# The last row tile of an encoder block: its last columns in two quarters, its last sum of squares on Vector, its scaling on three engines

## The chip, the cores and the metric

The kernel runs on one core of one Trainium2 chip. A core has five engines that run side by side, each with an instruction queue of its own: TensorE (PE; its weight loads are shown as PEld), VectorE (DVE), ScalarE (ACT), GpSimd (POOL) and SyncE (SP), which here only issues DMAs. ACT and POOL issue DMAs too. Engines wait for each other through semaphores. Matrix products go to PSUM, a small memory of eight banks (2 KB per partition each); all else is in SBUF, with 128 partitions.

The metric is the device time of one execution in microseconds, the median over runs. The kernel before takes 2623.02 us (three runs, 2622.14 to 2624.28).

## The reference

One encoder layer is applied to 512 prompt rows and 256 sample rows of width 2048. After a Fourier group, windowed attention, an output projection and a residual add comes the part that matters here:

```
h = rmsnorm(x, ln_mlp_g)
u = relu(h @ w_up)
x = x + (u * u) @ w_down        # w_down: 8192 x 2048
y = rmsnorm(x, ln_final_g)      # x * rsqrt(mean(x*x) + eps) * g
```

The last norm needs the sum of squares of a whole row of 2048 before any element of that row can be scaled.

## The kernel before

The 768 rows are six row tiles of 128 (`NM`). Everything is fp32; each matrix product is made of three fp32r products (high by high, high by low, low by high), since each factor is split into a high and a low part. The up and down projections use seven half-size products in place of eight (Strassen's scheme). For the down projection the list `dunits` has two halves `kh` of the inner dimension, seven products `i` in the order (4, 2, 6, 0, 1, 3, 5) and eight steps `j` each: 112 units. A unit multiplies three row tiles (m = 0, 1, 2) by 1024 columns, 12 matmuls of 512 columns for each m, into three PSUM tiles `ps` of two banks each. The pool of PSUM tiles has four such buffers.

TensorE's order is that of the program. The orders on the other engines, and the waits, come from a framework that follows the program's order where it can and adds a semaphore wait where data or a buffer needs one. PSUM is tracked by bank: a matmul into a bank waits for the reads of that bank that stand before it.

- `products` (L1343) issues the matmuls of one unit and one row tile; `start` and `stop` are set on the first and last of the group of eight steps.
- `lows` (L1337) and `sums` (L1319) prepare a unit's factors on Vector and Scalar one and two units ahead; `loads` (L1310) puts its DMAs on SP three units ahead.
- `evacuate` (L1428) adds a PSUM tile into `acc`, the result so far: one scalar_tensor_tensor on Vector (L1434), acc = ps * rm + acc. `acc4(m, n)` is row tile m, columns 512n to 512n + 511. `acc[r][0]` holds the left 1024 columns and `acc[r][1]` the right ones.
- `square` (L1268) is Scalar's Square with a sum along the row into `ssy`; `gains` (L1272) multiplies by `gf` (ln_final_g) on Vector.
- `row_factor` (L1277) reduces the four sums of a row tile on Vector, then `rsqrt_of` (L92) scales and adds eps on Vector (L94) and raises to the power -0.5 on GpSimd (L97).
- `put` (L1281) scales 512 columns, on Scalar (L1284) where the gain is already in and on Vector with `gf` (L1286) where it isn't, and issues the DMA of the result (L1289).

The final product (kh = 1, i = 5) changes only the right 1024 columns of row tiles 3, 4 and 5; the left columns of those are finished earlier, squared and multiplied by the gain beside the matmuls of the units before (`beside`, L1297). In the last two units the products of m = 2 are held back: after m = 0 and m = 1 of the last unit come 24 matmuls of 512 columns for m = 2 (L1442 to L1445), 12 for columns 1024 to 1535 and then 12 for 1536 to 2047. Behind them stands the tail, written out as a list (L1447): evacuate and square the two column blocks of a row tile, form its row factor, put its four blocks. The four result blocks of the last row tile go out by GpSimd's queue (columns 0 to 511), Scalar's (512 to 1023) and SP's (the two right ones). The framework ends the program with a drain of every engine and a barrier (shown at L1524, the line of the framework's context).

Of the kernel before, what the change touches and what calls it, by code (L numbers as in the profile page):

```python
# [11 lines left out]
F32 = mybir.dt.float32  # L12
# [8 lines left out]
P = 128  # L21
# [19 lines left out]
def hybrid_encoder(ctx: ExitStack, tc: tile.TileContext, a: dict):  # L41
# [1230 lines left out]
    def gains(m, n):  # L1272
        nc.vector.tensor_tensor(
            out=acc4(m, n), in0=acc4(m, n), in1=ep["gf"][:, n * 512 : (n + 1) * 512], op=ALU.mult
        )

    def row_factor(m):  # L1277
        nc.vector.tensor_reduce(out=ry[:, m : m + 1], in_=ssy[:, m * 4 : m * 4 + 4], op=ALU.add, axis=AX.X)
        rsqrt_of(ry[:, m : m + 1], ry[:, m : m + 1], D, 1)
# [62 lines left out]

    def products(u, ps, m, cols=range(2)):  # L1343
        _, i, j = dunits[u]
        (sh, sl, _), whl = parts[u]
        for n in cols:
            for q in range(2):
                ts, ns = slice(m * P, (m + 1) * P), slice(n * 512, (n + 1) * 512)
                wh, wl, _ = whl[q]
                for t, (l, w) in enumerate(((sh, wh), (sh, wl), (sl, wh))):  # L1350
                    nc.tensor.matmul(  # L1351
                        ps[m][:, ns], l[:, q, ts], w[:, ns],
                        start=(j == 0 and q == 0 and t == 0), stop=(j == HP // 2 - 1 and q == 1 and t == 2),
                    )
# [55 lines left out]
    for u, (kh, i, j) in enumerate(dunits):  # L1410
# [27 lines left out]
        for m in range(3 if u > 0 else 0):  # L1438

            if not (final and j >= HP // 2 - 2 and m == 2):  # L1440
                products(u, ps, m)
        if final and last:  # L1442
            for n in range(2):
                for v in (u - 1, u):
                    products(v, ps, 2, (n,))  # L1445

            for what, m, q in (  # L1447
# [3 lines left out]
            ):  # L1451
                if what == "e":
                    evacuate(m, q - 2)
                    square(3 + m, q)
                elif what == "r":
                    row_factor(3 + m)
                else:
                    put(3 + m, q, q < 2, {(2, 0): nc.gpsimd, (2, 1): nc.scalar}.get((m, q), nc.sync))
            parts.clear()
# [69 lines left out]
```

## Time and profile before

| | |
|---|---|
| median of three runs | 2623.02 us (2622.14 to 2624.28) |
| the profiled execution's own time | 2622.38 us |
| its span, first to last instruction | 2620.3 us |
| mean granted TensorE clock | 0.998 |
| busy PE / DVE / ACT / POOL | 99% / 66% / 41% / 10% |
| start of the last matmul | 2609.21 us of the span |
| from the end of the last matmul to the end of the span | 10.7 us |

The page of the profile gives busy times, a chain of waits followed back from the last instruction, and groups of like instructions. The timeline lists instructions in order of time: start, duration, engine, line, operation, out<-in, shape and type, how many merged into the row (x2: start of the first, time to the end of the last), and in brackets how long the engine was idle before and who ended it. A row with q behind the engine's name (SPq, POOLq) is that of its sequencer: it issues a DMA, waits or drains. Consecutive instructions of an engine overlap by some 0.08 us, so two of 0.75 us take 1.41 us together.

### The profile page before, as it was taken

To read this page: it belongs to the slowest core of one execution; us is meant where nothing else is said; L and a number is where in the kernel's file an instruction comes from. 1 tells how busy PE (TensorE), PEld (TensorE's weight loads), DVE (VectorE), ACT (ScalarE), POOL (GpSimd) and SP (SyncE) were. 2 spreads that over 40 slices of the span, in tenths; PEclk is the share of its full clock that TensorE was granted. 3 is DMA by queue.
4 is the path that set the end of the run, shared out by engine and by line. 5 is a ranking of instruction groups with operands and counts; after the bars stand their busy time and mean duration, and the time that the engine had idled before them with its cause. 6 is when DMAs were issued, how large, how long until landed. Compare 5 with 4: busy or idle time off the path is not lost.

```text
span 2620.3 us, 35122 instructions
## 1 busy us (share of the span) xinstructions
PE 2600.0 (99%) x13680; PEld 2378.5 (91%) x13680; DVE 1736.2 (66%) x2176; ACT 1075.8 (41%) x1543; POOL 251.8 (10%) x354
## 2 busy tenths in 40 slices
PE   9999999999999999999999999999999999999998
PEld 9999998887889999999999999988888888888886
DVE  6334447776655655555777777757776765777687
ACT  6233327775333333333454445433333333333335
POOL 1011212333210111000000000010000000000001
PEclk9999999999999999999999999999999999999999
DMA  5323466444673554456666666685543672555364
GB/s 179 120 94 111 136 216 181 117 121 145 208 240 137 174 179 162 155 202 232 208 227 213 220 228 225 208 324 181 184 157 110 211 246 78 178 179 162 98 210 147
DMA packets 254982, 465.16 MB, mean 178 GB/s; under 512 B 20080, under 2 KB 151712, under 8 KB 254176
## 3 DMA queue, kind: packets, MB, share of 16 engines
q1 hardware_dynamic: 189536, 304.24, 36.7%
q10 hardware_dynamic: 53376, 110.97, 11.2%
q0 software_dynamic: 11904, 47.72, 5.4%
q8 instruction: 107, 1.75, 0.3%
q14 instruction: 59, 0.48, 0.1%
HBM read 344.10 MB, written 118.75 MB: 177 GB/s over the span
## 4 chain that ended last, share of the span: by engine, by line
PE 75%; DVE 1%; DMA 1%; issue 0%; ACT 0%; POOL 0%; POOLq 0%; ACTq 0%; SPq 0%; DVEq 0%
PE pu L966 35%; PE pd L1351 34%; PE pm L821 5%; PE ptx L130 0%; DMA sr<-sd 0%; DMA sd<-sm 0%; DMA oar<-oad 0%; DVE sr L760 0%; POOL p L676 0%; DVE acc L1434 0%; ACT oar L756 0%; DVE wl L1340 0%; DVE os L720 0%; DVE tl L692 0%; DVE o L987 0%
## 5 line engine op out<-in xcount | busy, mean ns | idle before, releaser
L966 PE MATMUL pu<-xf,wh 128*128 128x384 f32 x3072 | 783.2, 336 | 0.0
L966 PEld LDWEIGHTS pu<-xf,wh 128*128 128x128 f32 x3072 | 554.6, 188 | 1.5 <-ACT o L984 0.8
L1351 PE MATMUL pd<-wh,sl 128*128 128x512 f32 x1332 | 518.3, 389 | 0.4 <-DVE sl L1341 0.4
L1351 PE MATMUL pd<-wh,sh 128*128 128x512 f32 x1332 | 518.2, 389 | 0.0
L1351 PE MATMUL pd<-wl,sh 128*128 128x512 f32 x1332 | 518.2, 389 | 0.0
L966 PE MATMUL pu<-xf,wl 128*128 128x384 f32 x1536 | 516.1, 336 | 0.0
L1330 ACT ACTIVATE wh<-rd 128x1024 fp32r<-128x1024 f32 x200 | 202.3, 1054 | 522.8 <-PE pd L1351 425.8
L1340 DVE TENSOR_TENSOR wl<-rd,wh 128x1024 fp32r<-128x1024 f32 x200 | 236.0, 1221 | 226.8 <-ACT wh L1330 226.1
L946 ACT ACTIVATE wh<-ur 128x1024 fp32r<-128x1024 f32 x160 | 169.9, 1062 | 372.5 <-PE pu L966 210.7
L1351 PEld LDWEIGHTS pd<-wh,sl 128*128 128x128 f32 x1332 | 250.1, 188 | 52.5 <-DVE sl L1341 0.8
L1351 PEld LDWEIGHTS pd<-wh,sh 128*128 128x128 f32 x1332 | 250.1, 188 | 51.9
L1351 PEld LDWEIGHTS pd<-wl,sh 128*128 128x128 f32 x1332 | 250.1, 188 | 51.9
L966 PEld LDWEIGHTS pu<-xf,wl 128*128 128x128 f32 x1536 | 288.8, 188 | 0.0
L952 DVE TENSOR_TENSOR wl<-ur,wh 128x1024 fp32r<-128x1024 f32 x160 | 195.4, 1222 | 76.2 <-ACT wh L946 76.2
L987 DVE TENSOR_TENSOR o<-pu,o 128x768 f32<-128x768 f32 x160 | 152.8, 956 | 122.5 <-PE pu L966 114.9
L588 PE MATMUL pz<-hh,wh 128*128 128x384 f32 x576 | 147.1, 336 | 0.0
L588 PE MATMUL pz<-hl,wh 128*128 128x384 f32 x576 | 146.3, 334 | 0.0
L588 PE MATMUL pz<-hh,wl 128*128 128x384 f32 x576 | 146.3, 334 | 0.0
L1323 DVE TENSOR_TENSOR rd<-rd 128x1024 f32<-128x1024 f32 x112 | 131.7, 1217 | 0.0
L966 PE MATMUL pu<-xs,wh 128*128 128x384 f32 x512 | 130.4, 336 | 0.0
L946 ACT ACTIVATE wh<-sx 128x1024 fp32r<-128x1024 f32 x64 | 67.9, 1062 | 130.4 <-PE pu L966 105.6
L66 DVE TENSOR_TENSOR wl<-raw,wh 128x1024 fp32r<-128x1024 f32 x56 | 68.3, 1225 | 69.4 <-ACT wh L65 69.1
(228 smaller groups left out, 3725.3 us busy)
## 6 DMA issues: line engine op xcount, KB each, us to landing
rd<-in_w_down SPq DMA_DIRECT2D x176, 512.0 KB, 5.1
ur<-in_w_up SPq DMA_DIRECT2D x128, 512.0 KB, 3.9
sr<-sd SPq DMA_DIRECT2D x95, 384.0 KB, 5.3
pd<-o ACTq DMA_DIRECT2D x60, 384.0 KB, 2.3
o<-pd POOLq DMA_DIRECT2D x60, 384.0 KB, 5.8
sd<-sm ACTq DMA_DIRECT2D x60, 384.0 KB, 2.9
raw<-in_w_in SPq DMA_DIRECT2D x40, 512.0 KB, 3.6
raw<-in_w_out SPq DMA_DIRECT2D x32, 512.0 KB, 4.5
```

The lines of the kernel that those rows point to most:

```text
L66: nc.vector.tensor_tensor(out=lo, in0=src, in1=f32(hi), op=ALU.subtract)
L588: nc.tensor.matmul(ps[c][s][:, :HALF], w[:, i, cs], h[j][:, i, s * HALF : (s + 1) * HALF], start=first and n == 0, stop=stop and n == 2,)
L821: nc.tensor.matmul(ps, l(k), w[:, k % 2, :], start=(k == 0 and n == 0), stop=(k == 7 and n == 2))
L946: nc.scalar.activation(wh[:], raw[:], AF.Copy)
L952: nc.vector.tensor_tensor(out=wl[:], in0=raw[:], in1=f32(wh[:]), op=ALU.subtract)
L966: nc.tensor.matmul(ps[:, t, :HALF], w[:, i, t * P : (t + 1) * P], xb[:, o, i, :], start=(s == first_of[bank] and i == 0 and n == 0), stop= ...
L987: nc.vector.tensor_tensor(out=o, in0=src, in1=o, op=ALU.add)
L1323: add = lambda x, y, op: nc.vector.tensor_tensor(out=x[:], in0=x[:], in1=y[:], op=op)
L1330: nc.scalar.activation(wh[:], t[:], AF.Copy)
L1340: nc.vector.tensor_tensor(out=wl[:], in0=t[:], in1=f32(wh[:]), op=ALU.subtract)
L1351: nc.tensor.matmul(ps[m][:, ns], l[:, q, ts], w[:, ns], start=(j == 0 and q == 0 and t == 0), stop=(j == HP // 2 - 1 and q == 1 and t == 2),)
```

## The change

The last row tile is r = 5 (m = 2). Its work at the end is taken out of the list and put into a generator, `last_rows`, whose steps the list calls at ("l", 2, ...).

- In unit j = 5 of the final product the group for columns 1536 to 2047 of m = 2 is closed, and in unit 6 Vector adds what it holds so far into `acc` (`take`).
- In the last unit come 12 matmuls of 512 columns for columns 1024 to 1535, as before; then 12 matmuls of 256 columns for 1536 to 1791 into a PSUM tile of their own, `pq` (the fourth buffer), and 12 of 256 columns for 1792 to 2047 into the second bank of `ps[2]`, which was emptied by that `take` in unit 6. These two groups hold only units 6 and 7.
- Each of the three pieces is added by `take` as it is done. Scalar squares the first (512) and the second (256); Vector reduces the four sums to `base`, scales it and adds eps; then the last quarter is squared and summed by one tensor_tensor_reduce on Vector, which starts from `base`. GpSimd's power follows.
- While GpSimd raises to the power, Vector multiplies columns 1024 to 1535 by the gain. Then Scalar scales columns 0 to 511, GpSimd 512 to 1023 and Vector both right blocks. Columns 0 to 511 go out by Scalar's queue, the other three by SP's.
- `base` is a new tile of one float per partition in the pool of constants; in the built program nearly all later SBUF tiles stand 32 bytes higher because of it.
- In the built program the order on Vector at the end is: `take` of columns 1024 to 1535, half of row tile 4's scaling, `take` of the first quarter, the other half of row tile 4's scaling, the reduce to `base` and its scaling, `take` of the last quarter, tensor_tensor_reduce, gain, two scalings. On Scalar: square (512), scaling of row tile 4's first block, square (256), scaling of its second block, scaling of columns 0 to 511.

```diff
+    def take(src, r, c0, sign=1):
+        w = src.shape[1]
+        y = acc[r][c0 // 1024][:, c0 % 1024 : c0 % 1024 + w]
+        nc.vector.scalar_tensor_tensor(
+            out=y, in0=src, scalar=(rm if sign > 0 else nrm)[:, r : r + 1], in1=y, op0=ALU.mult, op1=ALU.add
+        )
+
+    def last_rows(u, ps):
+
+        r = NM - 1
+        y, gf = acc[r][1], ep["gf"]
+        rc, base = ry[:, r : r + 1], stat("base", 1)
+        jk = ep["p"].tile([P, 512], F32, tag="jk", name="jk", bufs=1)
+        for v in (u - 1, u):
+            products(v, ps, 2, (0,))
+        yield
+        take(ps[2][:, :512], r, 1024)
+        nc.scalar.activation(jk[:], y[:, :512], AF.Square, accum_out=ssy[:, r * 4 + 2 : r * 4 + 3])
+        pq = pp.tile([P, 2, 512], F32, tag="ps", name="pdq")
+        outs = [pq[:, 0, :256], ps[2][:, 512:768]]
+        for v in (u - 1, u):
+            products(v, ps, 2, (512,), outs[0], HP // 2 - 2)
+        yield
+        take(outs[0], r, 1536)
+        nc.scalar.activation(jk[:, :256], y[:, 512:768], AF.Square, accum_out=ssy[:, r * 4 + 3 : r * 4 + 4])
+        for v in (u - 1, u):
+            products(v, ps, 2, (768,), outs[1], HP // 2 - 2)
+        yield
+        nc.vector.tensor_reduce(out=base[:], in_=ssy[:, r * 4 : r * 4 + 4], op=ALU.add, axis=AX.X)
+        nc.vector.tensor_scalar(out=base[:], in0=base[:], scalar1=1.0 / D, scalar2=EPS, op0=ALU.mult, op1=ALU.add)
+        take(outs[1], r, 1792)
+        nc.vector.tensor_tensor_reduce(
+            out=outs[0], in0=y[:, 768:], in1=y[:, 768:], scale=1.0 / D, scalar=base[:], op0=ALU.mult, op1=ALU.add, accum_out=rc,
+        )
+        nc.gpsimd.tensor_tensor(out=rc, in0=rc, in1=mhalf[:, :1], op=ALU.pow)
+        gains(r, 2)
+        x0, x1 = acc[r][0][:, :512], acc[r][0][:, 512:]
+        nc.scalar.activation(x0, x0, AF.Copy, scale=rc)
+        nc.vector.scalar_tensor_tensor(
+            out=y[:, 512:], in0=y[:, 512:], scalar=rc, in1=gf[:, 1536:], op0=ALU.mult, op1=ALU.mult
+        )
+        nc.gpsimd.tensor_scalar(out=x1, in0=x1, scalar1=rc, scalar2=1.0, op0=ALU.mult, op1=ALU.mult)
+        nc.vector.tensor_scalar(out=y[:, :512], in0=y[:, :512], scalar1=rc, scalar2=None, op0=ALU.mult)
+        nc.scalar.dma_start(out_rows(r)[:, :512], x0)
+        nc.sync.dma_start(out_rows(r)[:, 1536:], y[:, 512:])
+        nc.sync.dma_start(out_rows(r)[:, 512:1024], x1)
+        nc.sync.dma_start(out_rows(r)[:, 1024:1536], y[:, :512])
+        yield
...
-    def products(u, ps, m, cols=range(2)):
+    def products(u, ps, m, cols=(0, 512), out=None, j0=0, j1=NFF // 8 - 1):
...
-            if not (final and j >= HP // 2 - 2 and m == 2):
+            if final and j == HP // 2 - 3 and m == 2:
+                products(u, ps, m, (0,))
+                products(u, ps, m, (512,), j1=j)
+            elif not (final and j >= HP // 2 - 2 and m == 2):
                 products(u, ps, m)
+        if final and j == HP // 2 - 2:
+            take(ps[2][:, 512:], NM - 1, 1536)
         if final and last:
-            for n in range(2):
-                for v in (u - 1, u):
-                    products(v, ps, 2, (n,))
+            late = last_rows(u, ps)
+            next(late)
...
-                ("p", 0, 2), ("p", 0, 3), ("r", 1, 0), ("p", 1, 0), ("p", 1, 1), ("p", 1, 2), ("p", 1, 3), ("e", 2, 2),
-                ("e", 2, 3), ("r", 2, 0), ("p", 2, 0), ("p", 2, 1), ("p", 2, 2), ("p", 2, 3),
+                ("p", 0, 2), ("p", 0, 3), ("r", 1, 0), ("l", 2, 0), ("p", 1, 0), ("p", 1, 2), ("l", 2, 1),
+                ("p", 1, 1), ("p", 1, 3), ("l", 2, 2),
```

More of the change, by code (lines that the diff above doesn't have):

```diff
@@ L1341, in lows @@
         nc.vector.tensor_tensor(out=sl[:], in0=sr[:], in1=f32(sh[:]), op=ALU.subtract)
-    def products(u, ps, m, cols=range(2)):
+    def products(u, ps, m, cols=(0, 512), out=None, j0=0, j1=NFF // 8 - 1):
         _, i, j = dunits[u]
         (sh, sl, _), whl = parts[u]
-        for n in cols:
+        for c0 in cols:
+            o = ps[m][:, c0 : c0 + 512] if out is None else out
             for q in range(2):
-                ts, ns = slice(m * P, (m + 1) * P), slice(n * 512, (n + 1) * 512)
+                ts, ns = slice(m * P, (m + 1) * P), slice(c0, c0 + o.shape[1])
                 wh, wl, _ = whl[q]
@@ L1351, in products @@
                     nc.tensor.matmul(
-                        ps[m][:, ns], l[:, q, ts], w[:, ns],
-                        start=(j == 0 and q == 0 and t == 0), stop=(j == HP // 2 - 1 and q == 1 and t == 2),
+                        o, l[:, q, ts], w[:, ns],
+                        start=(j == j0 and q == 0 and t == 0), stop=(j == j1 and q == 1 and t == 2),
                     )
@@ L1457, in hybrid_encoder @@
                 else:
-                    put(3 + m, q, q < 2, {(2, 0): nc.gpsimd, (2, 1): nc.scalar}.get((m, q), nc.sync))
+                    put(3 + m, q, q < 2)
             parts.clear()
```

4 lines of the change are left out of this document (3 added, 1 removed).

## The prediction

> **What bounds the kernel now.** I read the head of the page and the chain of waits first, then the timeline of the last 12 us, then the drains and the landings of the last DMAs.
>
> ```profile
> span 2620.3 us, 35122 instructions
> PE 2600.0 (99%) x13680; PEld 2378.5 (91%) x13680; DVE 1736.2 (66%) x2176; ACT 1075.8 (41%) x1543; POOL 251.8 (10%) x354
> ...
> PE 75%; DVE 1%; DMA 1%; issue 0%; ACT 0%; POOL 0%; POOLq 0%; ACTq 0%; SPq 0%; DVEq 0%
> ```
>
> TensorE is busy 99% of the span and is 75% of the chain that ended last. The change removes no product, so all that it can shorten is what follows the last matmul.
>
> The timeline of the end (start, duration, engine, line):
>
> ```profile
> 2608.99 0.39 PE L1351 MATMUL pd<-wl,sh 128*128 128x512 f32 x1
> 2609.21 0.39 PE L1351 MATMUL pd<-wh,sl 128*128 128x512 f32 x1
> 2609.64 1.41 DVE L1434 SCALAR_TENSOR_TENSOR acc<-pd,rm,acc 128x512 f32<-128x512 f32 x2 [0.38 <-PE pd L1351]
> ...
> 2611.77 0.19 ACT L1270 ACTIVATION_READ_ACCUMULATOR jk<-acc 128x1 f32 x1
> ...
> 2612.18 0.15 DVE L94 TENSOR_SCALAR ry<-ry 128x1 f32<-128x1 f32 x1
> 2612.41 0.55 POOL L97 TENSOR_TENSOR ry<-ry,mhalf 128x1 f32<-128x1 f32 x1 [4.61 <-DVE ry L94]
> 2613.00 1.34 ACT L1284 ACTIVATE acc<-acc,ry 128x512 f32<-128x512 f32 x2 [1.04 <-POOL ry L97]
> 2613.00 1.41 DVE L1286 SCALAR_TENSOR_TENSOR acc<-acc,ry,gf 128x512 f32<-128x512 f32 x2 [0.66 <-POOL ry L97]
> 2614.02 0.59 POOL L1289 DMA_DIRECT2D out_y_sample<-acc  x1 [1.05 <-ACT acc L1284]
> 2614.36 0.37 ACTq L1289 DMA_DIRECT2D out_y_sample<-acc  x1
> ```
>
> The last matmul starts at 2609.21 and ends at 2609.60. From there one thing follows another: two additions on Vector (1.41 us), two squares on Scalar behind them (the second reads its sum out at 2611.96), a reduce, a scaling, GpSimd's power (ends 2612.96), four scalings in two pairs (until 2614.41), and the DMAs.
>
> The drains that end the program, and the landings of the last DMAs (count, KB, us from issue to landing; SP's is the first of the last four, issued at 2613.78):
>
> ```profile
> L1524 POOLq DRAIN  x3: 40/102/5566, 2614.0 to 2620.1; - x3
> L1524 SPq DRAIN  x3: 7/7/7, 2618.4 to 2619.8; - x3
> L1524 ACTq DRAIN  x2: 8/80/153, 2614.8 to 2619.8; - x2
> ```
>
> ```profile
> 2613.78 0.33 SPq L1289 DMA_DIRECT2D out_y_sample<-acc  x1
> ```
>
> ```profile
> out_y_sample<-acc POOLq DMA_DIRECT2D x1, 256.0 KB, 3.2
> out_y_sample<-acc ACTq DMA_DIRECT2D x1, 256.0 KB, 3.7
> out_y_sample<-acc SPq DMA_DIRECT2D x1, 256.0 KB, 2.2
> ```
>
> Scalar's DMA is issued at 2614.36 and lands 3.7 us later, at 2618.06: 4.28 us after the first of the last four was issued (2613.78). SP, which waits for all landings, drains at 2618.4. But GpSimd's drain, begun at 2614.0, lasts 5.57 us, until 2619.56; only then comes the barrier, and the span ends at 2620.3. So two things end the program: the landings, and 1.1 us later GpSimd's drain.
>
> **The change part by part.** *Matmuls.* 12 of 512 columns become 24 of 256. The trace has 256-column matmuls in fp32r elsewhere:
>
> ```profile
> 49.59 0.52 PE L232 MATMUL pv<-wh,hl 128*128 128x256 f32 x3
> 49.59 0.88 PE L232 MATMUL pv<-wh,hl 128*128 128x256 f32 x6
> ```
>
> Six end 0.36 us after the first three of them (asked for in two windows): 0.12 us each, which is the time from start to start, against (2609.21 - 2604.00) / 23 = 0.2265 for the 24 of 512 (the first is shown in the next fence). The first 12 run from 2604.00 as before, the next starts at 2606.72, the last of 24 at 2606.72 + 23 x 0.12 = 2609.48, and with its 0.28 us (0.52 - 2 x 0.12) it ends at 2609.76: a loss of **0.16 us**.
>
> *The early addition.* Vector adds 512 columns in unit 6.
>
> ```profile
> 2596.98 1.28 DVE L1273 TENSOR_TENSOR acc<-acc,gf 128x512 f32<-128x512 f32 x2
> 2601.48 1.41 DVE L1434 SCALAR_TENSOR_TENSOR acc<-pd,rm,acc 128x512 f32<-128x512 f32 x2 [3.22 <-PE pd L1351]
> 2604.00 0.39 PE L1351 MATMUL pd<-wh,sh 128*128 128x512 f32 x1
> 2606.43 2.75 ACT L1284 ACTIVATE acc<-acc,ry 128x512 f32<-128x512 f32 x4
> 2607.03 0.15 DVE L94 TENSOR_SCALAR ry<-ry 128x1 f32<-128x1 f32 x1
> 2607.26 0.55 POOL L97 TENSOR_TENSOR ry<-ry,mhalf 128x1 f32<-128x1 f32 x1 [2.45 <-DVE ry L94]
> 2607.84 1.42 DVE L1286 SCALAR_TENSOR_TENSOR acc<-acc,ry,gf 128x512 f32<-128x512 f32 x2 [0.66 <-POOL ry L97]
> ```
>
> It comes behind the gain that ends at 2598.26, where Vector was idle 3.22 us, and takes 0.75 us (as one of the two additions at 2601.48): nothing. Without that cover the evacuation at 2601.48 would move by 0.75 us, with slack behind it. The first matmul for m = 2 waits for this addition, five microseconds after it is done. The matmuls into the second bank wait for nothing newer than the addition of columns 1024 to 1535 (done at 2607.95, below), and TensorE arrives at 2606.72 + 12 x 0.12 = 2608.16: no stall, with 0.2 us to spare.
>
> *Vector and Scalar before the last quarter.* Durations for 256 columns, from groups by line and form (mean ns after the comma):
>
> ```profile
> L646 DVE CUSTOM_DVE_ANT_0 p<-s,mask,sink 128x256 f32<-128x256 f32 x64 | 30.4, 476 | 5.9 <-PE s L631 4.1 <-PE t L688 1.8
> ...
> L646 DVE DVE_READ_ACCUMULATOR2_ANT mx<- 128x1 f32 x96 | 7.8, 81 | 0.0
> ...
> L69 DVE SCALAR_TENSOR_TENSOR vhl<-pv,r,vhl 128x256 fp32r<-128x256 f32 x7 | 3.3, 478 | 1.7 <-ACT vhl L68 1.7
> ```
>
> ```profile
> L65 ACT ACTIVATE ah<-pa 128x256 fp32r<-128x256 f32 x24 | 9.1, 378 | 34.5 <-PE pa L392 34.5
> ```
>
> Vector is free at 2607.18. It adds 512 columns until 2607.95, scales half of row tile 4 until 2608.62 (power at 2607.81, no wait), adds the first quarter (478 ns) until 2609.02, scales the other half until 2609.69. Scalar's two scalings of row tile 3 end about 2607.77 (two take 1.34 us); its square of 512 runs 2608.04 to 2608.67, row tile 4's first block to 2609.38, the square of 256 (378 ns) to 2609.68, its sum is out at 2609.78. **The added wait**: the reduce to `base` stands on Vector ahead of the last addition and waits for that sum. Reduce and scaling end at 2610.15, so the last quarter, ready at 2609.76, is taken only from 2610.17 to 2610.65. Behind it the sum of squares (476 + 81 ns, overlapped) ends at 2611.17. Before, the corresponding point (the scaling by L94) was 2612.33. The chain up to here is **1.16 us** shorter: one quarter's addition in place of two additions of 512, and a half-microsecond square in place of two with their read-outs.
>
> *The power, with the gain beside it.* Vector starts the gain (two SBUF inputs; 0.68 us, as one of the two at 2596.98) at 2611.10, just before GpSimd can start (0.08 us behind the sum). The trace shows what that does:
>
> ```profile
> 2583.34 2.35 DVE L1323 TENSOR_TENSOR rd<-rd 128x1024 f32<-128x1024 f32 x2
> 2583.51 1.46 POOL L97 TENSOR_TENSOR ry<-ry,mhalf 128x1 f32<-128x1 f32 x1 [7.91 <-DVE ry L94]
> ```
>
> With two Vector additions of two SBUF tiles running ((2.35 + 0.08) / 2 = 1.22 us each), the power took 1.46 us and ended at 2584.97, 0.41 us after the first of them ended (2584.56); at 2607.26, with Vector idle, it took 0.55. So I let the power end at 2611.78 + 0.41 = 2612.19 and not at 2611.25 + 0.55 = 2611.80. The part gives back **0.39 us**; the power is 0.77 us earlier than the 2612.96 of before.
>
> The Trainium skill ("SBUF — State Buffer", section "Who interferes with whom") has this as a rule: a Vector instruction with two SBUF inputs and a GpSimd instruction that reads SBUF exclude each other, and the second to issue waits for the first to end. The rows agree that it waits; by the rule to the letter the power would end at 2612.33, 0.14 us later, since the rows show only 0.41 of its 0.55 us behind the blocker.
>
> *The scalings.* They start at 2612.22. Scalar's ends at 2612.95 and Vector's first, with two SBUF inputs, at 2612.97. GpSimd's 512 columns have no row; the nearest has 256 and 384 columns (ns: least, median, most):
>
> ```profile
> L676 POOL TENSOR_SCALAR p<-p,rs x96: 472/481/1602, 408.5 to 611.3; 128x256 f32<-128x256 f32 x64, 128x384 f32<-128x384 f32 x32
> ```
>
> The median of 481 ns is near the least, which is 256 columns; twice that is 0.96 us, and 1.6 us is the longest. Between 0.5 and 1.6 us, I take 0.7, nearer to the median, begun when Vector's first is done: 2613.7. Vector's second (one input, 512) is bounded by 0.15 (one column, L94) and 0.68 (the gain); near the latter, behind GpSimd or ahead of it, it ends between 2613.6 and 2614.3.
>
> *The DMAs.* Scalar issues at 2612.98, SP at 2613.0, then SP's other two at about 2613.7 and 2614.2, in that order. The last of these can land 2.2 us after its issue, at 2616.4; but four pieces of 256 KB need their time on the DMA engines. With the 4.28 us of before, all have landed at 2612.98 + 4.28 = 2617.26: **0.80 us** earlier. If SP's last issue slipped to 2615, that gain would be gone.
>
> *GpSimd's drain.* GpSimd issues no DMA at the end any more. Its drain of 5.57 us followed its own DMA; Scalar also had issued one, which landed later still, and Scalar's drain took at most 0.15 us. So a landing isn't what a drain waits for; what is left is that GpSimd's DMA itself keeps its drain. Between 0 and **1.1 us** I take 1.1: the drain of SP is then the last.
>
> **Sum:** 0.80 + 1.1 = 1.9 us. The profiled execution takes 2622.38 us, of which the span is 2620.3; it would take 2620.5. It stands 0.64 below the median, to which I apply the same difference: 2623.02 - 1.9 = **2621.1 us**.
>
> **The rivals.** *The drain stays.* If GpSimd's drain has its length for another reason than the DMA, only the landings count: 2623.02 - 0.8 = 2622.2. For it: one drain with one DMA is all that the trace has. Against it: Scalar's 0.15 us.
>
> *The power isn't held up.* If GpSimd starts ahead of the gain, or the gain doesn't block it, all behind is 0.4 us earlier: 2620.7. For it: only 0.15 us lie between the two starts (2611.10 and 2611.25).
>
> *The shifted addresses: slower.* `base` moves nearly all tiles by 32 bytes. The matmuls can't be the victims:
>
> ```profile
> L966 PE MATMUL pu<-xf,wh 128*128 128x384 f32 x3072 | 783.2, 336 | 0.0
> L588 PE MATMUL pz<-hh,wh 128*128 128x384 f32 x576 | 147.1, 336 | 0.0
> ```
>
> `xf` already stands 224 bytes past a multiple of 256 in the built program and `hh` at 0, with the same 336 ns. But DMAs might be longer everywhere. They are 1% of the chain, 26 us; from 7% more on (1.9 / 26) the gain is eaten, and at a tenth the kernel takes 2623.02 + 2.6 - 1.9 = 2623.7. Over 5.2 us (0.2%) it would need 27%. Against it stands a pair of equal size and queue, whose SBUF tile is at 0 (`zs`) and at 32 (`of`):
>
> ```profile
> zf<-zs ACTq DMA_DIRECT2D x8, 384.0 KB, 2.3
> ofd<-of ACTq DMA_DIRECT2D x8, 384.0 KB, 2.3
> ```
>
> Both land in 2.3 us, so at most a few per cent, and most loads are issued units ahead of their use. The Trainium skill ("DMA: Bandwidth & Descriptors", section "How a descriptor splits into AXI transactions") speaks for this rival: a descriptor that doesn't start at a multiple of 256 bytes pays for one more transaction. By that an estimate for a row of 4 KB is 17 in place of 16, 6%, just under the point that decides.
>
> **How the numbers follow.** The forecast 2621.1 has 0.50, the drain that stays 0.27, the free power 0.13, the shift 0.10. The runs of before spread from 0.9 below the median to 1.3 above. The range goes from the free power less that spread and less 0.4 us, half of the 0.86 by which the last landing could come before 2617.26, so from 2620.7 - 0.9 - 0.4 = 2619.4, to the drain that stays with the spread, 2623.5, and the shift at a tenth, 2623.7. All of this is less than 0.2% (5.2 us), about what a measurement of this kernel can tell from no change: 10.7 us lie behind the last matmul in all. Faster by over 0.2% has 0.02, slower 0.03 (of the shift's 0.10), between 0.95.
>
> **What the profile of the changed kernel would show.** The last matmul ends about 2609.76; the last addition on Vector starts near 2610.17, behind the reduce and not behind TensorE; GpSimd's last power takes 0.9 us and not 0.55; all landings by 2617.3; GpSimd's drain short, and the span about 2618.4. A power of 0.55, a drain that ends over a microsecond behind SP's, or matmul starts further apart than 0.227 anywhere would show which step was wrong. A gain or loss over 5 us would mean that something outside the tail moved.

## The result, and the profile after

The kernel after the change takes 2634.32 us at the median of 22 runs (2622.67 to 2640.01); the kernel before takes 2622.86 us beside it (22 runs, 2620.35 to 2626.67). The ratio is 1.0040, 95% interval 1.0031 to 1.0049: slower by 11.5 us, where 2621.1 and a gain of 1.9 us had been forecast. The runs of before lie within 6.3 us, those of after spread over 17.3.

The profiled execution of the change is the fastest of its 22, 2622.67 us. It shows the new tail well and the loss hardly, so a second execution of the same kernel was profiled later (e13, 2636.86 us). First the head of the page of the first one:

```profile
span 2620.9 us, 35151 instructions
## 1 busy us (share of the span) xinstructions
PE 2600.9 (99%) x13692; PEld 2380.0 (91%) x13692; DVE 1737.7 (66%) x2181; ACT 1074.8 (41%) x1542; POOL 251.4 (10%) x354
```

The 12 added matmuls are there (13692 against 13680), and the span is 0.6 us longer than before, not 1.9 shorter. The timeline of its end:

```profile
2608.84 0.28 PE L1401 MATMUL pdq<-wh,sh 128*128 128x256 f32 x1
...
2611.59 0.28 PE L1401 MATMUL pd<-wh,sl 128*128 128x256 f32 x1
2611.61 0.19 ACT L1301 ACTIVATION_READ_ACCUMULATOR jk<-acc 128x1 f32 x1
...
2611.83 0.16 DVE L1305 TENSOR_REDUCE base<-ssy 128x1 f32<-128x4 f32 x1
2612.02 0.15 DVE L1306 TENSOR_SCALAR base<-base 128x1 f32<-128x1 f32 x1
2612.09 0.47 DVE L1280 SCALAR_TENSOR_TENSOR acc<-pd,rm,acc 128x256 f32<-128x256 f32 x1
...
2613.01 0.14 DVE L1308 DVE_READ_ACCUMULATOR2_ANT ry<- 128x1 f32 x1
2613.01 0.69 DVE L1273 TENSOR_TENSOR acc<-acc,gf 128x512 f32<-128x512 f32 x1
2613.23 0.87 POOL L1311 TENSOR_TENSOR ry<-ry,mhalf 128x1 f32<-128x1 f32 x1 [3.30 <-DVE ry L1308]
...
2614.21 1.24 POOL L1318 TENSOR_SCALAR acc<-acc,ry 128x512 f32<-128x512 f32 x1
2614.81 0.92 DVE L1319 TENSOR_SCALAR acc<-acc,ry 128x512 f32<-128x512 f32 x1
2614.89 0.37 ACTq L1320 DMA_DIRECT2D out_y_sample<-acc  x1
...
2615.90 0.75 SPq L1323 DMA_DIRECT2D out_y_sample<-acc  x1
```

Everything is some two microseconds later than forecast because TensorE arrives later: its last matmul ends at 2611.87 (2611.59 + 0.28), before at 2609.60. From there to the end of the span it is 9.0 us, against 10.7 before. So the tail did become shorter, by 1.7 us, and TensorE lost 2.3 us ahead of it. (The second profile of the change has the same 9.0 us.) The drains that close the program (in each row the duration's least, median and most in ns; first and last start in us):

```profile
L1580 POOLq DRAIN  x3: 40/93/5967, 2614.1 to 2620.6; - x3
L1580 SPq DRAIN  x3: 7/7/7, 2619.5 to 2620.4; - x3
L1580 DVEq DRAIN  x2: 19/824/1630, 2614.2 to 2620.4; - x2
```

SP's drain, behind the last landing, comes at 2619.5. GpSimd's, begun at 2614.1, lasts 5.97 us, until 2620.1, although GpSimd issues no DMA any more. It still ends last, 0.65 us behind SP's where it was 1.12 in before: of the forecast's 1.1 us of gain 0.5 is there.

Where TensorE loses time is seen in the up projection (L966), 900 us ahead of the edited lines. Its moving tiles are `xf` and `xs`, the second factor in the code, and its stationary tiles `wh` and `wl`, the ones that the LDWEIGHTS rows load. One row of the groups of that line in before, in the first profile of the change and in the second (count; duration of one in ns; first and last start):

```profile
L966 PE MATMUL pu<-xf,wl x1536: 336/336/338, 761.3 to 1694.6; 128*128 128x384 f32 x192
```

```profile
L966 PE MATMUL pu<-xf,wl x1536: 333/335/339, 760.7 to 1696.7; 128*128 128x384 f32 x192
```

```profile
L966 PE MATMUL pu<-xf,wl x1536: 334/338/343, 762.1 to 1711.0; 128*128 128x384 f32 x192
```

The same 5376 matmuls of this line take 933.3 us before, 936.0 in the first profile of the change and 948.9 in the second. The windows of TensorE show how (us; busy us with the count of matmuls; granted clock; DMA share; GB/s), of before, then of the first profile of the change, then of the second:

```profile
780.00:850.00 70.00, 70.00 (x406) 1.00 0.44 150
850.00:1000.00 150.00, 150.00 (x865) 1.00 0.49 165
...
1113.00:1500.00 387.00, 387.00 (x2234) 1.00 0.64 217
...
2300.00:2590.00 290.00, 290.00 (x1281) 1.00 0.50 163
```

```profile
780.00:850.00 70.00, 70.00 (x398) 1.00 0.43 148
850.00:1000.00 150.00, 150.00 (x864) 1.00 0.49 165
...
1113.00:1500.00 387.00, 387.00 (x2233) 1.00 0.64 216
```

```profile
780.00:850.00 70.00, 70.00 (x403) 1.00 0.46 156
850.00:1000.00 150.00, 150.00 (x853) 1.00 0.49 163
...
1113.00:1500.00 387.00, 387.00 (x2193) 1.00 0.63 213
...
2300.00:2590.00 290.00, 290.00 (x1281) 1.00 0.49 163
```

TensorE is busy without a gap and its clock is full in every row; there are just fewer matmuls in the same time. 387 us for 2234 of them are 173.2 ns from the start of one to the start of the next, which is called the pitch here; for 2193 they are 176.5. In the first profile only stretches are slow (70 us for 398: 175.9 ns), in the second nearly all. The down projection behind it (2300 to 2590) has the same count in both. Nothing in L966 is edited. What the change does to it is the one thing that the tile `base` does at compile time: it moves the stationary tiles `wh` and `wl` by 32 bytes, while the moving tiles `xf` and `xs`, which are laid out from the other end of SBUF, stay.

### The profile page after: what moved, and what is told of

Same layout as the page of the kernel before. It is cut to its first block, busy times and chain, and to the rows that moved or that the text cites. A ratio compares the mean times of both kernels' runs of the same rounds, so it can differ in the third digit from the quotient of the medians.

```text
span 2620.9 us, 35151 instructions
## 1 busy us (share of the span) xinstructions
PE 2600.9 (99%) x13692; PEld 2380.0 (91%) x13692; DVE 1737.7 (66%) x2181; ACT 1074.8 (41%) x1542; POOL 251.4 (10%) x354
## 4 chain that ended last, share of the span: by engine, by line
PE 75%; DVE 1%; DMA 1%; ACT 0%; issue 0%; POOL 0%; ACTq 0%; DVEq 0%; SPq 0%; POOLq 0%
PE pu L966 35%; PE pd L1401 34%; PE pm L821 5%; PE ptx L130 0%; DMA sr<-sd 0%; DMA sd<-sm 0%; DVE sr L760 0%; DMA oar<-oad 0%; PE o L707 0%; DVE acc L1484 0%; DVE wl L1389 0%; DVE tl L692 0%; DVE o L987 0%; ACT o L994 0%; ACT o L995 0%
## 5 line engine op out<-in xcount | busy, mean ns | idle before, releaser
L966 PE MATMUL pu<-xf,wh 128*128 128x384 f32 x3072 | 783.3, 336 | 0.0
L966 PEld LDWEIGHTS pu<-xf,wh 128*128 128x128 f32 x3072 | 555.2, 188 | 0.9 <-ACT o L984 0.6
L966 PE MATMUL pu<-xf,wl 128*128 128x384 f32 x1536 | 515.6, 336 | 0.0
L966 PEld LDWEIGHTS pu<-xf,wl 128*128 128x128 f32 x1536 | 288.2, 188 | 0.0
L588 PE MATMUL pz<-hh,wh 128*128 128x384 f32 x576 | 147.1, 336 | 0.0
L588 PE MATMUL pz<-hl,wh 128*128 128x384 f32 x576 | 146.3, 334 | 0.0
L588 PE MATMUL pz<-hh,wl 128*128 128x384 f32 x576 | 146.3, 334 | 0.0
L966 PE MATMUL pu<-xs,wh 128*128 128x384 f32 x512 | 130.2, 335 | 0.0
```

The lines of the kernel that those rows point to most:

```text
L588: nc.tensor.matmul(ps[c][s][:, :HALF], w[:, i, cs], h[j][:, i, s * HALF : (s + 1) * HALF], start=first and n == 0, stop=stop and n == 2,)
L966: nc.tensor.matmul(ps[:, t, :HALF], w[:, i, t * P : (t + 1) * P], xb[:, o, i, :], start=(s == first_of[bank] and i == 0 and n == 0), stop= ...
```

## The experiments

Two theories at first. **A**: the loss is the addresses; the edited instructions themselves save about what their tail shows. **B**: the new tail, or its instructions, cost the time. Each kernel ran in five rounds beside the kernel before on the same chip (median there 2622.20 for e1 to e4, 2621.74 for e5 to e8, 2621.83 for e9 to e12); e13 and e14 have one execution each.

**e1, the shift alone.** The kernel before with an unused tile behind `nrm`:

```diff
     nrm = stat("nrm")
+    pad = stat("pad", 1)
```

> The kernel before with one more tile of one float per partition (32 bytes with its padding) in the pool of constants, used by nothing: all large tiles stand where they stand after the change. Theory A (the addresses cost the time, the new tail gains): slower than before by 10 us or more, about 2634 to 2636 us, with runs spread over 10 us or more, and stretches of the up projection whose matmuls of 384 columns start 176 to 178 ns apart and not 173 to 174. Theory B (the new tail costs the time): as before, 2623 us within 1.5, spread under 7 us.

Measured: 2635.59 us (9 runs, 2624.11 to 2638.59), ratio 1.0038 [1.0024, 1.0053]. An unused tile of one float, 32 bytes with its padding, costs what the whole change costs, with the same wide spread. Its profiled execution (2631.50 us) loses the time in the same stage, 941.8 us:

```profile
L966 PE MATMUL pu<-xf,wl x1536: 333/338/340, 761.8 to 1703.6; 128*128 128x384 f32 x192
```

**e2, the change without the shift.** The scalar is kept in a column of a tile that exists:

```diff
-        rc, base = ry[:, r : r + 1], stat("base", 1)
+        rc, base = ry[:, r : r + 1], r0[:, :1]
```

> The whole change, but `base` is a column of a tile that is free by then, so that every large tile stands where it stood before. Theory A (addresses): 2621.2 us within 1, that is 1.7 us faster than before (the profile after shows 9.05 us from the last matmul to the end against 10.70), spread as before. Theory B (the new tail): 2634 us with a wide spread, as after the change.

Measured: 2619.82 us (11 runs, 2617.30 to 2624.93), ratio 0.9992 [0.9984, 1.0001]. Without the shift the loss is gone, and the medians lie 2.4 us apart in favour of the change, an interval from 4.2 us faster to 0.3 slower. The up projection takes the 933.3 us of before:

```profile
L966 PE MATMUL pu<-xf,wl x1536: 336/336/340, 760.2 to 1693.5; 128*128 128x384 f32 x192
```

A holds, B falls.

**e3 and e4, other shifts.** As e1 with pads of 64 and 128 bytes (`stat("pad", 16)`, `stat("pad", 32)`).

> The kernel before with a pad of 64 bytes. If what counts is a tile's place modulo 64 bytes: as before, 2623 us within 1.5. If it is the place modulo 256 bytes, or any move: slower by 5 us or more, 2628 to 2640 us, with a wide spread. Theory B: as before.

> The kernel before with a pad of 128 bytes. Modulo 64 or 128 bytes: as before, 2623 us within 1.5. Modulo 256 bytes or any move: slower by 5 us or more, with a wide spread. Theory B: as before.

Measured: 64 bytes 2624.91 us (11 runs), ratio 1.0011 [1.0001, 1.0021], with one run of the eleven at 2636.02 and the others up to 2626.32; 128 bytes 2639.95 us (5 runs), ratio 1.0066 [1.0054, 1.0078]. So it isn't that everything has to stand at a multiple of 64 or 128: a shift by 128 is the worst and one by 64 next to harmless. The up projection of e4:

```profile
L966 PE MATMUL pu<-xf,wl x1536: 336/338/347, 762.7 to 1712.9; 128*128 128x384 f32 x192
```

950.2 us against 933.3, 16.9 of the 17.8 us by which the medians differ.

**e5 to e7, which address matters.** Three theories: (1) the distance between moving and stationary tile, (2) the place of the tiles that other engines and the DMAs use, against the moving tile, (3) the place of the stationary tile alone. All distances here are addresses modulo 256, moving tile less stationary tile; 256 is a way to write them, and that they repeat with it was not tested. e5 puts 128 bytes behind the weights, so that they stay and the later pools move; e6 moves the moving tiles down by 128; e7 does that together with e4's pad. In code, behind `nrm` and behind `xf` in turn:

```diff
+    pad = wpool.tile([P, 32], F32, tag="pad", name="pad", bufs=1)     # e5
+    xpad = tp.tile([P, 32], F32, tag="xpad", name="xpad")             # e6, e7
+    pad = stat("pad", 32)                                             # e7
```

> The kernel before with a 128-byte pad behind the weights' tiles in their pool: the stationary tiles (wh, wl) of the up projection stay at 0 past a multiple of 256 and the moving ones (xf, xs) at 224, while every tile of the later left pools (ur, sx, o, sm, acc) moves by 128 as in e4_pad128. Theory 1 (the distance between moving and stationary tile sets the pitch of the matmuls): as before, 2622 us, 173.3 ns from one L966 matmul to the next. Theory 2 (the place of the tiles that other engines and DMAs use, against the moving tile): as e4_pad128, 2640 us, 176 to 177 ns. Theory 3 (the place of the stationary tile by itself, whatever the moving tile's): as before, 2622 us.

> The kernel before with a 128-byte pad in the pool of xf: the moving tiles of the up projection go down by 128, from 224 to 96 past a multiple of 256, the stationary ones stay at 0. Theory 1 (distance): the same distance modulo 256 as in e4_pad128, so 2640 us and 176 to 177 ns. Theory 2 (other engines' tiles against the moving tile): 2640 us too. Theory 3 (stationary tile alone): 2622 us, 173.3 ns. If theory 3 held and e5 were slow as well, none of the three would be right.

> Both pads: the stationary tiles at 128 as in e4_pad128 and the moving ones at 96 as in e6. Theory 1: the distance modulo 256 is again that of before, so 2622 us and 173.3 ns. Theory 2: 2622 us as well. Theory 3 (stationary tile alone): 2640 us, 176 to 177 ns.

Measured: e5 2649.75 us (4 runs), ratio 1.0105 [1.0091, 1.0119]; e6 2639.49 us (5 runs), 1.0068 [1.0054, 1.0082]; e7 2623.99 us (11 runs), 1.0006 [0.9997, 1.0015]. By the times alone (1) and (3) miss e5, and only (2) comes near (2640 expected). The traces say otherwise. The up projection in e5, in e6 and in e7 (one more line above it in the last two):

```profile
L966 PE MATMUL pu<-xf,wl x1536: 333/336/339, 765.2 to 1698.5; 128*128 128x384 f32 x192
```

```profile
L967 PE MATMUL pu<-xf,wl x1536: 336/338/347, 761.1 to 1711.3; 128*128 128x384 f32 x192
```

```profile
L967 PE MATMUL pu<-xf,wl x1536: 336/336/340, 763.0 to 1696.3; 128*128 128x384 f32 x192
```

933.3, 950.2 and 933.3 us: in e5 the up projection is as fast as before, with all other engines' tiles moved, so (2) is out; in e7 the stationary tile stands where it did in e4 and all is well, so (3) is out. (1) holds for the up projection in all three. What e5's expectation had overlooked is that other products have one tile in the weights' pool and the other in a later one, and their distance did change. One row of the down projection in before, and in e5:

```profile
L1351 PE MATMUL pd<-wh,sl x1332: 388/389/504, 1704.0 to 2609.2; 128*128 128x512 f32 x191
```

```profile
L1352 PE MATMUL pd<-wh,sl x1332: 390/393/498, 1707.9 to 2635.9; 128*128 128x512 f32 x191
```

928.0 us against 905.2: 22.8 us lost in a stage that e4 had left alone (there both of its tiles move together). With 4 us of L588, whose matmuls go from 334 to 337 ns, that makes up 27 of e5's 28 us. In both lines the distance is 0 in before and 128 in e5. So (1) predicted the pitch of L966 rightly and the time of e5 wrongly, and the same rule explains the miss.

**e8 and e9, the tail.** Both start from e2. e8 scales columns 512 to 1023 on Scalar; e9 besides drops the gain beside the power and issues that DMA from Scalar:

```diff
-        gains(r, 2)                                                            # e9
-        nc.gpsimd.tensor_scalar(out=x1, in0=x1, scalar1=rc, ...)
+        nc.scalar.activation(x1, x1, AF.Copy, scale=rc)
-        nc.vector.tensor_scalar(out=y[:, :512], in0=y[:, :512], scalar1=rc, ...)   # e9
+        nc.vector.scalar_tensor_tensor(out=y[:, :512], in0=y[:, :512], scalar=rc, in1=gf[:, 1024:1536], ...)   # e9
-        nc.sync.dma_start(out_rows(r)[:, 512:1024], x1)                        # e9
+        nc.scalar.dma_start(out_rows(r)[:, 512:1024], x1)                      # e9
```

> The change without its shift (as e2_change_no_shift), with columns 512 to 1023 scaled by Scalar instead of GpSimd, so that GpSimd's last instruction is the power, some 1.3 us earlier. Theory: GpSimd's drain ends 4.7 us behind its last instruction, DMA or not; it then ends some 1.3 us earlier, about with SP's, and the span ends 0.8 to 1.2 us earlier than in e2_change_no_shift: 2618.8 us. Rival: the drain waits for something else (the landings): as e2, 2619.8 us, with the drain ending 0.8 us or so behind SP's. GpSimd's drain in the profile tells the two apart where the time can't.

> As e8_scaled_by_two_engines, and: no gain beside the power (Vector's second scaling multiplies by the gain itself), and Scalar instead of SP issues the DMA of columns 512 to 1023. Theory (the gain holds the power up; GpSimd's drain ends 4.67 us behind its last instruction): the power takes 0.55 us and not 0.87, starts right behind the sum of squares, and GpSimd's drain ends 4.67 us behind it; SP's last landing comes 0.9 us earlier against the sum of squares than in e8; from the end of the sum of squares to the end of the span 0.9 us less than in e8's profile. The time: some 2619.0 us. Rival: the power takes 0.87 us even with nothing beside it, or the drain is longer.

Measured: e8 2620.36 us (11 runs), ratio 0.9994 [0.9985, 1.0002]; e9 2618.57 us (11 runs), ratio 0.9987 [0.9978, 0.9996]. e8 can't be told from e2 by its time, and the 2618.8 us that were expected are missed; in the profiles its tail is shorter, 8.30 us from the last matmul to the end against 9.03 in e2. Its timeline and drains, then those of e9:

```profile
2614.58 0.87 POOL L1311 TENSOR_TENSOR ry<-ry,mhalf 128x1 f32<-128x1 f32 x1 [3.30 <-DVE ry L1308]
```

```profile
L1580 POOLq DRAIN  x3: 40/93/5577, 2614.5 to 2621.2; - x3
L1580 SPq DRAIN  x3: 7/7/7, 2620.7 to 2621.0; - x3
```

```profile
2610.10 0.55 POOL L1311 TENSOR_TENSOR ry<-ry,mhalf 128x1 f32<-128x1 f32 x1 [3.29 <-DVE ry L1308]
```

```profile
L1581 POOLq DRAIN  x3: 40/102/5254, 2610.1 to 2616.4; - x3
L1581 SPq DRAIN  x3: 7/7/7, 2615.9 to 2616.2; - x3
```

In e8 GpSimd's drain ends at 2620.1, 4.67 us behind the power (2615.45); in e9 at 2615.3, 4.67 behind the power (2610.65); in the change 4.67 behind its scaling (2615.45 to 2620.12). The profiles of e2, e10 and e13 have the same 4.67 behind the scaling. So without a DMA the drain ends a fixed time behind GpSimd's last instruction. That is not the whole rule: in the ten profiles in which GpSimd issues a DMA at the end, of before and of before with a pad, the drain ends 2.38 us behind the landing of that DMA, and moves with it. In before the DMA is issued at 2614.02 and lands at 2617.18, and the drain ends at 2619.56; in e1 they are 2622.95, 2626.28 and 2628.65, and the drain is the longer by 0.16 us:

```profile
L1525 POOLq DRAIN  x3: 40/102/5725, 2622.9 to 2629.2; - x3
```

With the scaling gone the drain ends ahead of SP's in e8 and e9. Without the gain beside it the power takes 0.55 us and not 0.87. Of e9's expectation one part failed: from the end of the sum of squares to that of the span it is 6.7 us, after 7.0 in e8, 0.36 us and not 0.9. The first of the last four DMAs is issued at 2616.24 in e8 and the last lands 4.18 us later; in e9 it is 2611.44 and 4.15. The four pieces need that time whichever queue issues them, so only the earlier power is left as a gain. e9 is faster than both kernels: by 0.13% against before, interval 0.04 to 0.22, the only one of the intervals that lies wholly below 1.

**e10, the change with its tile made 64 bytes wide.**

```diff
-        rc, base = ry[:, r : r + 1], stat("base", 1)
+        rc, base = ry[:, r : r + 1], stat("base", 16)
```

(and `base[:, :1]` where it is used)

> The change as it is, with base made 64 bytes wide instead of 4, so that the stationary tiles stand at 64 and not at 32 past a multiple of 256 (the moving ones stay at 224, distance 160 as in e3_pad64). Theory (the distance sets the pitch; the change itself is harmless): 173.3 ns from one up-projection matmul to the next, 2620 us, as e2_change_no_shift. Rival (the tile as such, or its instructions, cost time): as the change, 2634 us.

Measured: 2622.30 us (11 runs, 2620.36 to 2624.94), ratio 1.0001 [0.9992, 1.0010]. The loss and the wide spread are gone with a larger tile in the same place. A gain like that of e2 (0.9992) doesn't show here, but the two intervals overlap, and by the times what the new tail is worth by itself is known no closer than they say. The profiles are closer: from the last matmul to the end it is 9.03 us in e2, in e10 and in e13, 9.04 in the first profile of the change, and 10.73 to 10.90 in the ten profiles of the old tail. The tail is 1.7 us shorter, of which the added matmuls take back about 0.15 ahead of it (the 24 of 256 columns take 3.03 us, 12 of 512 would take 12 x 0.2265 + 0.16 = 2.88).

**e11 and e12, other distances.** The moving tiles moved down by 32 and by 160 bytes (`xpad` of 8 and of 40 columns).

> The kernel before with xf and xs moved down by 32 bytes, to 192 past a multiple of 256; all the left tiles stay. The distance to the stationary tiles is 192, as in the change and in e1_pad32. Theory (distance alone): a mean pitch between 174 and 177 ns that changes from stretch to stretch, 2626 to 2638 us. Rival (what was slow in e1_pad32 came from where the other engines' tiles stood): 173.3 ns, 2622 us.

> The kernel before with xf and xs moved down by 160 bytes, to 64 past a multiple of 256: a distance of 64, that no run has had. Known so far, distance modulo 256 and pitch of the 384-column matmuls: 0, 160 and 224: 173.3 ns; 192: 174 to 177; 96 and 128: 176 to 177. The theory says that the distance decides and not which distances are slow; by the neighbour (96) it is slow: 2640 us. If only the distances near 128 are slow: 2622 us.

Measured: e11 2635.20 us (5 runs), ratio 1.0048 [1.0036, 1.0061]; e12 2622.71 us (11 runs), ratio 0.9999 [0.9990, 1.0008]. e11 has the distance of the change with all tiles but the moving ones where they stood before, and is as slow. e12 was expected slow by its neighbour (96) and is fast: only the distances and their effect are known, not the rule behind them. The table has the distance of the moving behind the stationary tile modulo 256, for matmuls of 384 columns; the pitch is the mean of the profile from start to start, in the up projection from 780 to 1690 us (in L588 from one of its own matmuls to the next, breaks of over 200 ns left out).

| distance | seen in | up projection, us | pitch, ns |
|---|---|---|---|
| 0 | before, L588 | | 173.5 |
| 64 | e12 | 933.3 | 173.5 |
| 96 | e4, e6 | 950.2, 950.2 | 176.7 |
| 128 | e5, L588 | | 175.8 |
| 160 | e3, e10 | 933.2, 933.7 | 173.5, 173.6 (one run of e3's 11 slow) |
| 192 | the change, e13, e1, e11 | 936.0, 948.9, 941.8, 948.2 | 174.0 to 176.3, by stretches |
| 224 | before, e2, e5, e7 | 933.3 in each | 173.5 |

**e13, the change profiled once more.** Its rows stand above.

> The change as it is, profiled once more. Theory (the up projection's matmuls at distance 192 are the whole loss): whatever this execution takes, its time above that of e2_change_no_shift (2619.4 profiled) is the sum, over the windows of the up projection from 780 to 1690 us, of the extra pitch times the matmuls: at 2634 us some 14.6 us, a mean pitch of 176.1 ns over the 5250 matmuls; the 512-column windows behind it keep 226.6 ns. Rival (something else is slow in the typical execution): the pitch is as in the first profile, 173 to 174 ns in most windows, and the loss stands elsewhere.

Measured: 2636.86 us. Against the profile of before, the span is 14.8 us longer (2635.1 and 2620.3): the up projection begins 0.8 us later, takes 15.6 us more, the stages from there to the last matmul take the same 915.0 us, and the tail 1.7 less, which adds up to it within 0.1. The pitch from 780 to 1690 us is 176.3 ns, in before 173.5. So the up projection holds the whole loss. Against e2, which the expectation names, the span is 17.4 us longer: 15.6 in the up projection and 1.9 ahead of it, where profiles of kernels at fast distances differ by more (the up projection begins at 759.0 in e9 and at 764.4 in e8).

**e14, only one of the two stationary tiles at a slow distance.** The pad stands between `wh` and `wl`, which puts `wl` alone at 96:

```diff
+    padded = []
+
...
         hi = wpool.tile(raw.shape, F32R, tag="wh", name="wh", bufs=4)
+        padded or padded.append(wpool.tile([P, 32], F32, tag="pad", name="pad", bufs=1))
```

> The kernel before with the 128-byte pad between the tiles wh and wl, so that in the up projection wh stays at distance 224 from the moving tile (fast) and wl goes to 96 (slow). Of three matmuls with the same weights (wh, wh, wl in this order) theory Q (the load of the next stationary tile collides with the moving tile's reading) lengthens the second, during which wl is loaded; theory P (a matmul's own stationary tile) lengthens the third. Either way a third of the matmuls goes from 173.3 to 176.7 ns, a mean of 174.4 ns. If all three stay at 173.3 or all go to 176.7, neither holds. All tiles behind the weights move by 128 too, as in e5, so that the other products slow down in part as there: the time itself, 2640 to 2660 us, tells nothing.

Measured: 2644.68 us in its one execution. Its timeline:

```profile
1299.88 0.36 PEld L969 LDWEIGHTS pu<-xs,wh 128*128 128x128 f32 x2
1300.04 0.52 PE L969 MATMUL pu<-xs,wh 128*128 128x384 f32 x2
1300.22 0.19 PEld L969 LDWEIGHTS pu<-xs,wl 128*128 128x128 f32 x1
1300.40 0.33 PE L969 MATMUL pu<-xs,wl 128*128 128x384 f32 x1
1300.40 0.19 PEld L969 LDWEIGHTS pu<-xs,wh 128*128 128x128 f32 x1
```

The matmuls begin with the loads that run beside them: the first with `wh` at 1300.04, the second at 1300.22, the one with `wl` at 1300.40, and the next follows at 1300.57. Between 1150 and 1480 us, over some 625 of each kind, the starts lie 175.8 ns apart behind the first, 180.0 behind the second and 170.9 behind the one with `wl`; in before it is 173.0, 173.4 and 173.6. So the matmul beside which `wl` is loaded grows by 6.6 ns, and the one that multiplies by `wl` does not grow at all. Theory Q holds in its main point and P falls. It is not the whole story: the first also grows by 2.8 ns and the third shrinks by 2.7, and the mean is 175.6 and not 174.4. With one tile of two at the slow distance, two thirds of the loss of e4 are there (in the same stretch e4 has 176.7 ns, before 173.3), where Q expects one third. Whether the load or the running matmul waits for the other these starts don't tell.

The Trainium skill ("TensorE: Matmul & The Clock Gate", section "Step-by-step: what each phase is for") says that "Loading the next tile's weights doesn't steal SBUF read bandwidth from the running matmul." This trace does not bear that out at a distance of 96: behind the matmul beside the load the next one starts after 180.0 ns instead of 173.4.

What stays open is why these distances collide and others don't, and why a distance of 192 is fast in some stretches and executions and slow in others (up projections of 936.0 and 948.9 us from the same program). At 160 one of e3's eleven runs was as slow as those at 192. A distance of 32 was not tried.

## Why the prediction was wrong

- **The step that failed** is "The matmuls can't be the victims" under the shifted addresses. It compared `xf` at 224 and `hh` at 0, found 336 ns for both, and took from that that an address does not matter to a matmul. Both rows are of before, where the stationary tiles stand at 0: they show two distances that are fast, and the change makes a third one, 192. The step looked at the tile that doesn't move, not at the pair. It also went by the duration of one matmul, which in e13 is 338 ns and not 336, and not by the pitch, 176.3 and not 173.5. With the matmuls ruled out, the rival was priced on the DMAs, 26 us of the chain, of which a tenth was 2.6 us. Its true base was the 933.3 us of the up projection, of which 1.7% are the 15.6 us seen in e13. That the range ended at 2623.7 and "slower" got 0.03 both follow from this.
- The last part named both signs that came: "matmul starts further apart", there with the down projection's 0.227 in mind, where nothing moved, and that a loss over 5 us would mean something outside the tail.
- **The DMAs under the shifted addresses.** What the rival put on the DMAs is there, but only at the end of the program: the last four pieces take 4.31 us from the first issue to the last landing in the change and 4.30 in e10, where e2 and e8 without a shift take 4.18; with the old tail it is 4.47 to 4.51 with a pad ahead of `acc` and 4.28 to 4.30 without. That is 3 to 5% of them, 0.1 to 0.2 us; the loads of the weights show nothing of the kind (`rd`, 4.8 to 5.1 us to landing with and without a shift).
- **GpSimd's drain, 1.1 us**, was the second failure. "So a landing isn't what a drain waits for" rested on Scalar's 0.15 us alone, and for GpSimd it is wrong: its drain ends 2.38 us behind the landing of its own DMA. "What is left is that GpSimd's DMA itself keeps its drain" is right for before; what the step had not seen is that the drain is long without a DMA too, and then ends 4.67 us behind GpSimd's last instruction. That instruction became the scaling, and the drain still ends last.
- **The tail as a whole** came out between the forecast and its rival. From the last matmul to the end 8.64 us were forecast (2618.4 - 2609.76), with the drain that stays 9.74; measured are 9.03, because the drain also ends earlier than before: 8.24 us behind the last matmul against 9.96. That both 2621.1 and the rival's 2622.2 lie between the 2619.82 of e2 and the 2622.30 of e10, the two kernels that have the new tail without the loss, decides nothing.
- **Landings, 0.80 us**: right in size, in part by luck. 4.28 us were taken from the first issue to the last landing; it is 4.31 (2614.89 to 2619.20), but e2 with the same four pieces and no shift has 4.18. SP's last issue is at 2615.90, 4.03 us behind the last matmul; 4.44 were worked out (2614.2 - 2609.76), and 5.24 (2615) was the point from which the prediction saw the gain gone, so that sign was not put to the test. Taken from the last matmul, all has landed 1.1 us earlier than before, with 0.96 (0.80 and the 0.16 of the matmuls) worked out.
- **The power beside the gain, 0.39 us given back**: right in cause and near in size. It took 0.87 us and ended 0.40 behind the gain (2614.10 and 2613.70); in e9, without the gain, it took 0.55, so 0.32 was given back.
- **The matmuls of 256 columns**: right. The 24 run from 2608.84 to 2611.59 + 0.28, 3.03 us; worked out were 23 x 0.12 + 0.28 = 3.04.
- **The added wait**: right. The last quarter is taken at 2612.09 behind reduce and scaling, 0.22 us behind the last matmul (0.41 worked out: Scalar's read-out came 0.09 us earlier against the last matmul, and the addition began 0.08 before the scaling ended).
- **GpSimd's scaling** ended 1.35 us behind the power, with 1.5 worked out. Its row begins at once and lasts 1.24 us, but it stands beside Vector's first scaling, which has two SBUF inputs, began 0.07 us earlier and ended at 2614.89; from there to the end of GpSimd's it is 0.56 us, where 0.7 behind Vector's first was worked out. How much of the 1.24 us is waiting the trace doesn't say. Vector's second scaling took 0.92 us beside it, and in e8, where GpSimd scales nothing, 0.48:

```profile
2616.16 0.48 DVE L1319 TENSOR_SCALAR acc<-acc,ry 128x512 f32<-128x512 f32 x1
```

## What to carry to other kernels

A new tile of a few bytes is an edit of every product of which it moves one operand and not the other: compare the built programs' addresses, and for each busy matmul line the distance between moving and stationary tile modulo 256, before a tail is costed in tenths. Where a whole stage gets slower without a gap, with a full clock and no line edited, count the matmuls in equal windows. Two groups that are equally fast at two addresses show that these pairs are fast; they don't show that addresses don't matter.

## What the runs showed of the hardware

- The address distance between the moving tile of a matmul and the stationary tile that is loaded beside it changes the pitch: 173.5 to 176.7 ns at 384 columns (before and e4), and 226.4 to 232.0 at 512 (290 us over 1281 matmuls in before's window from 2300 to 2590, over 1250 in e5's). The shown duration of one moves only from 336 to 338 ns at 384 columns, and the clock not at all.
- The same program can be fast or slow at one distance (192): executions of the change lie between 2622.67 and 2640.01 us, where at 224 the kernel before stays within 2620.35 to 2626.67.
- GpSimd's drain at the end of the program ends 4.67 us behind its last instruction in the six profiles in which that is no DMA (the change, e2, e8, e9, e10, e13), and 2.38 us behind the landing of its own last DMA in the ten others. Vector's, in the change, ends 0.05 us behind Vector's last instruction (2615.78 and 2615.73). Why GpSimd's takes so long is not shown. The Trainium skill ("VectorE: DVE Perf Modes", section "The DRAIN you can't avoid") gives the drains of the program's frame as some 12 ns on all engines; SP's 7 ns come near that, GpSimd's 5.97 us and Vector's 1.63 us don't.
- The last four result pieces of 256 KB take 0.1 to 0.2 us longer in all when the tiles they are read from are moved by 32, 64 or 128 bytes (4.18 to 4.31 us, 4.28 to 4.51).
